# Ranking eight experts by token count and running three of them with both token parts in one stationary operand

## The chip, the core and the metric

The kernel runs on one core of one Trainium2 chip. The core has TensorE (PE in the rows; PEld is its weight load), VectorE (DVE), ScalarE (ACT), GpSimd (POOL) and SyncE (SP, which here issues the weight loads). The metric is the device time of one execution in microseconds (us). Before the change it is 1649.99 us, the median of three runs (1649.68 to 1650.12).

## The reference, cut to what matters

256 tokens of width 1024 go through two layers. Each layer has a mixer (attention, a gated delta rule and projections); the first is followed by a dense feed-forward part, the second by a mixture of eight experts. Only the experts are touched by the change:

```python
logits = xt @ router_w + router_b                    # 256 x 8
top_val, top_idx = lax.top_k(logits, 2)              # two experts for each token
gates = jax.nn.softmax(top_val, axis=-1)
# for each expert e, on the tokens that chose it:
gt, up = jnp.split(h @ w_gate_up[e], 2, axis=-1)     # 1024 -> 2 x 3584
y = (jax.nn.silu(gt) * up) @ w_down[e]               # 3584 -> 1024
x[token] += gate * y
```

Each expert holds 42 MiB of float32 weights, 336 MiB in all, and every expert's weights are used once. On the inputs of this case the reference's routing gives experts 0 to 7 these token counts: 42, 78, 96, 70, 54, 47, 76, 49.

## The kernel before

**Products in parts.** A float32 product is made of TensorE passes on a rounded type: a weight w is split into wh (rounded, written by ScalarE) and wl = w - wh (written by VectorE), and the activations likewise into a high and a low part. Three passes are added up in PSUM: high x wh, high x wl, low x wh. The activation is the stationary operand (128 columns: up to 128 tokens of one expert), the weights stream as 512 moving columns.

**Units and chunks.** A weight is loaded in units of 1 MiB (128 x 2048) by SyncE (`load`, L163 to L175). An expert has 7 chunks of 512 hidden columns; a chunk has 6 units: two of the gate half, two of the up half, two of the down projection. Each unit takes 12 matmuls, that is three for each of its four 128 x 512 blocks. `Weights` (L1023) keeps the order of units: `take(i)` asks for wh up to unit i+3 and wl up to unit i+2. Raw units have 12 buffers (NRAW = 5 and seven blocks), wh has 4 and wl has 3. A raw buffer comes free when its wl is written, so a load is issued then; a wl buffer comes free when TensorE has done the unit's matmuls.

**The loop over experts** (L1319 to L1344) runs expert after expert, chunk after chunk, in a fixed order on TensorE, ScalarE and VectorE (`pin`). For chunk c: the gate matmuls into pg (`gu`, L1239); ScalarE's silu of it to egt (L1325); the up matmuls into pu; VectorE's product egt (L1327); the down matmuls of the chunk before it into py (`finish`, `down`, L1250); four transposes of egt into pet (L1332); ScalarE's eah and VectorE's eal, the two parts of the turned activations (L1335, L1336).

**Tokens in and out.** `gather(e)` at chunk 1 builds a one-hot matrix GM from the tokens' slots (L1194), gets row numbers and gates by a small float32 matmul (pheld), and GpSimd fetches the expert's rows by an indirect transfer (xg, L1211). `turn` at chunk 4 transposes them to hTe in two parts. After an expert's last chunk `add_rows` scales py on ScalarE to ys and GpSimd adds the rows to acc in DRAM (L1270). Expert 0 gets its tokens by matmuls with GM, and experts 0 and 7 give their results back by matmuls (`scatter`). `gates` (L1158) makes the gates and the largest token count; if any expert has more than 128 tokens, the whole loop runs a second time for the rest (L1349).

Of the kernel before, what the change touches and what calls it, by code (L numbers as in the profile page):

```python
# [11 lines left out]
F32 = mybir.dt.float32  # L12
F32R = mybir.dt.float32r
# [5 lines left out]
P = 128  # L19
# [6 lines left out]
BESIDE = 16  # L26
# [17 lines left out]
K_COLS = K_KEPT + K_LEV + 128 * len(LEVELS)  # L44


def shape_constants():
# [10 lines left out]
    c[:, K_TOK:K_TOK + 4] = np.arange(P)[:, None] + np.array([0, P, S, 0])  # L58
    m = c[:, K_KEPT:]
# [8 lines left out]
class Even:  # L68
# [5 lines left out]
    def tile(self, shape, dtype, past=0, **kw):  # L74
        n = math.prod(shape[1:])
        if past:
            return self.pool.tile([shape[0], n + 64], dtype, **kw)[:, past:past + n].rearrange("p (a b) -> p a b", a=shape[1])
        return (self.small if n % 64 else self.pool).tile(shape, dtype, **kw)


def build(ctx, tc, nc, A, out, upto=99):
# [290 lines left out]
    def turned(pool, w, name, past=0):  # L372


        hh = pool.tile([P, KD, S], F32R, past=past, tag="hh", name=f"hh_{name}")
        hl = pool.tile([P, KD, S], F32R, past=past, tag="hl", name=f"hl_{name}")
# [73 lines left out]
    def mixer(l, mp):  # L450
# [500 lines left out]
        M = mp.tile([P, K_COLS - K_KEPT], F32, name="M")  # L951
        if l == 0:
            late_constants()
        nc.sync.dma_start(M, A["consts"][:, K_KEPT:])
# [6 lines left out]
    def ffn(l, fp):  # L961
        wg, wd = A["ffn_w_gate_up"], A["ffn_w_down"]
        with tc.high_priority():
            act = turned(fp, cols[:, V_FFN + 8 * l:V_FFN + 8 * l + 8], f"ffn{l}", 64 - BESIDE)
            _, rB = scales(fp)
# [49 lines left out]
    def moe(l, ep, wp, dram):  # L1015
# [7 lines left out]
        class Weights:  # L1023
# [36 lines left out]

        def sources(order):
            srcs, prev = [], None
            for e in order:
                wg, wd = A["moe_w_gate_up"][e], A["moe_w_down"][e]
                for c in range(nch):
                    srcs += [wg[2 * c + i] for i in range(2)] + [wg[14 + 2 * c + i] for i in range(2)] + (prev or [])
                    prev = [wd[2 * c + i] for i in range(2)]
            return srcs + prev

        W = Weights(sources(range(E)), "e")  # L1070
        W.hi(1, "c6")
        with tc.high_priority():
# [9 lines left out]
            xs = [ep.tile([P, D], F32, tag=f"xs{b}", name=f"xs{b}") for b in range(NB)]  # L1082
# [16 lines left out]
            def scores(b, n):  # L1099
# [6 lines left out]
                sq = ep.tile([P, 512], F32, tag="eah", bufs=2, name="nsq")  # L1106
# [40 lines left out]
        gate = ep.tile([P, NB, E], F32, name="gate")  # L1147

# [9 lines left out]
        def gates():  # L1158
            pcn = psb([P, E], "pcn")
            for b in range(NB):  # L1160
                mm(pcn, ones, sel[:, b, :], b == 0, b == NB - 1)
            cmax = ep.tile([P, 1], F32, name="cmax")
            V.tensor_reduce(cmax, pcn, axis=AX.X, op=ALU.max)
# [8 lines left out]
            V.tensor_tensor(gate, ex, mx[:, :, None].to_broadcast([P, NB, E]), op=ALU.mult)  # L1172
# [4 lines left out]
        def experts(off):  # L1177
            sl, xt = slot, xs
            if off:
                sl = ep.tile([P, NB, E], F32, name="slot2")  # L1180
                V.tensor_scalar(sl, slot, float(off), None, op0=ALU.subtract)
                xt = [ep.tile([P, D], F32, tag=f"xs{b}", name=f"xt{b}") for b in range(NB)]
                for b in range(NB):
                    nc.sync.dma_start(xt[b], xd[b * P:(b + 1) * P, :])
            ws = Weights(sources(range(E)), "o") if off else W
            used = [0]

            def gather(e):

                GM = ep.tile([P, NB, NS], F32, tag="GM", bufs=3, name="GM")  # L1190
                early = not off and e == 0
                for b in range(NB):
                    place = slot0[:, b, :] if early else sl[:, b, e:e + 1]
                    V.tensor_tensor(GM[:, b], iota0 if early else iota, place.to_broadcast([P, NS]), op=ALU.is_equal)  # L1194
                xg = rows = None
                if not off and e:

                    ph = psb([P, 3], "pheld")
                    for b in range(NB):
                        mm(ph, GM[:, b], held[:, b, e, :], b == 0, b == NB - 1)  # L1200
                    rows = ep.tile([P, 3], F32, tag="rows", bufs=3, name="rows")
                    V.tensor_copy(rows, ph)
                    ri = ep.tile([P, 2], I32, tag="ri", bufs=3, name="ri")
# [7 lines left out]
                    G.indirect_dma_start(out=xg, out_offset=None, in_=xd[:, :],  # L1211
                                         in_offset=bass.IndirectOffsetOnAxis(ap=ri[:, 0:1], axis=0))
# [227 lines left out]
```

## Time and profile before

| what | value |
|---|---|
| median of 3 runs | 1649.99 us |
| the profiled execution, its own time | 1650.56 us |
| its span, first to last instruction | 1648.8 us |
| TensorE busy in the span | 98% |
| VectorE busy | 82% |
| ScalarE busy | 65% |
| first gate matmul of expert 0 | 671.78 us after the span's start |
| mean rate of DMA, 800 to 1600 us | 380 GB/s |

The first 672 us are the two mixers, the dense part and the router; the last 977 us are the experts. In the rows each line is a group or a stretch of instructions: where a time stands first it counts from the span's start. TensorE's matmuls overlap, so the step from one start to the next, not the duration, tells how long one holds the engine.

### The profile page before, as it was taken

What the parts mean: (1) busy time and instruction counts of PE and PEld (TensorE: products, weight loads), DVE (VectorE), ACT (ScalarE), POOL (GpSimd) and SP (SyncE); (2) the same over time, 40 slices, a digit from 0 to 9 for tenths busy, and PEclk for the clock granted to TensorE, in tenths of its full rate; (3) what the DMA queues carried; (4) which work ended last, traced back from release to release, by engine and by line L of the source; (5) the groups of instructions that cost most, each with busy time, mean ns of one, the idle gap of its engine ahead of it and who ended that gap; (6) DMA issues with size and microseconds to landing.
All of it is one profiled execution on the core that took longest, in us unless ns stands there. A gap on an engine that the chain in (4) does not pass through costs nothing. (4 is left out here: it accounts for less than half of the span.)

```text
span 1648.8 us, 23472 instructions
## 1 busy us (share of the span) xinstructions
PE 1617.3 (98%) x9198; PEld 1402.8 (85%) x9198; DVE 1353.7 (82%) x1491; ACT 1069.4 (65%) x1124; POOL 96.3 (6%) x70
## 2 busy tenths in 40 slices
PE   8999999999999999899999999999999999999997
PEld 6899999999889997788788888888888888888885
DVE  6998776655799876789988888888888888888885
ACT  7555454444645554577777777777777777777773
POOL 0510000000051000000000000000100100000000
PEclk9999999999999999899999999999999999999998
DMA  7423455555442564699999999999999999999970
GB/s 291 156 100 143 155 185 197 180 189 195 142 140 103 183 252 155 258 375 370 365 391 358 383 397 364 382 391 370 381 390 364 393 382 356 408 365 376 400 308 28
DMA packets 67511, 466.61 MB, mean 283 GB/s; under 512 B 8000, under 2 KB 8512, under 8 KB 12608
## 3 DMA queue, kind: packets, MB, share of 16 engines
q1 hardware_dynamic: 64080, 453.95, 72.2%
q0 software_dynamic: 2160, 7.87, 1.7%
q10 hardware_dynamic: 1152, 3.21, 0.5%
q8 instruction: 74, 1.21, 0.3%
q14 instruction: 45, 0.37, 0.1%
HBM read 458.18 MB, written 6.82 MB: 282 GB/s over the span
## 5 line engine op out<-in xcount | busy, mean ns | idle before, releaser
L1052 DVE TENSOR_TENSOR wl_e<-raw,wh_e 128x2048 fp32r<-128x2048 f32 x336 | 753.4, 2284 | 7.5 <-PE pg L1237 1.8
L1039 ACT CAST wh_e<-raw 128x2048 fp32r<-128x2048 f32 x335 | 641.4, 1915 | 127.6 <-PE py L1237 37.8
L1237 PE MATMUL pg<-wh_e,hTe 128*128 128x512 f32 x896 | 293.0, 398 | 3.1 <-DVE hTe L1228 3.1
L1237 PE MATMUL pu<-wh_e,hTe 128*128 128x512 f32 x896 | 284.9, 389 | 0.0
L1237 PEld LDWEIGHTS pg<-wh_e,hTe 128*128 128x128 f32 x896 | 168.9, 189 | 38.6 <-DVE hTe L1228 3.7
L1237 PEld LDWEIGHTS pu<-wh_e,hTe 128*128 128x128 f32 x896 | 168.2, 188 | 34.9
L1237 PE MATMUL py<-wh_e,eal 128*128 128x512 f32 x448 | 175.3, 391 | 2.1 <-DVE eal L1336 2.1
L1237 PE MATMUL pg<-wl_e,hTe 128*128 128x512 f32 x448 | 175.8, 392 | 0.0
L1237 PE MATMUL py<-wh_e,eah 128*128 128x512 f32 x448 | 175.0, 391 | 0.5 <-ACT eah L1335 0.5
L1237 PE MATMUL py<-wl_e,eah 128*128 128x512 f32 x448 | 174.9, 390 | 0.0
L1237 PE MATMUL pu<-wl_e,hTe 128*128 128x512 f32 x448 | 174.3, 389 | 0.0
L1237 PEld LDWEIGHTS py<-wh_e,eal 128*128 128x128 f32 x448 | 84.5, 189 | 20.1 <-DVE eal L1336 2.6
L1237 PEld LDWEIGHTS py<-wh_e,eah 128*128 128x128 f32 x448 | 84.5, 189 | 18.2 <-ACT eah L1335 0.7
L1237 PEld LDWEIGHTS py<-wl_e,eah 128*128 128x128 f32 x448 | 84.5, 189 | 17.6
L1237 PEld LDWEIGHTS pu<-wl_e,hTe 128*128 128x128 f32 x448 | 84.1, 188 | 17.4
L318 PE MATMUL pf<-hh_ffn,wl_fg 128*128 128x256 f32 x352 | 98.8, 281 | 0.0
L1237 PEld LDWEIGHTS pg<-wl_e,hTe 128*128 128x128 f32 x448 | 84.7, 189 | 16.6 <-DVE wl_e L1052 0.3
L318 PE MATMUL pf<-hh_ffn,wh_fg 128*128 128x256 f32 x352 | 98.8, 281 | 0.0
L318 PE MATMUL pf<-hl_ffn,wh_fg 128*128 128x256 f32 x352 | 98.7, 281 | 0.0
L1336 DVE TENSOR_TENSOR eal<-pet,eah 128x512 fp32r<-128x512 f32 x56 | 38.7, 690 | 66.5 <-ACT eah L1335 66.5
L154 DVE TENSOR_TENSOR wl_fg<-raw,wh_fg 128x1024 fp32r<-128x1024 f32 x44 | 53.8, 1225 | 41.1 <-ACT wh_fg L153 41.0
L153 ACT CAST wh_fg<-raw 128x1024 fp32r<-128x1024 f32 x44 | 46.1, 1049 | 63.8 <-PE pf L318 37.5
(410 smaller groups left out, 2981.0 us busy)
## 6 DMA issues: line engine op xcount, KB each, us to landing
raw<-moe_w_gate_up SPq DMA_DIRECT2D x224, 1024.0 KB, 7.3
raw<-moe_w_down SPq DMA_DIRECT2D x112, 1024.0 KB, 7.7
raw<-w_in SPq DMA_DIRECT2D x43, 1024.0 KB, 4.8
raw<-ffn_w_gate_up SPq DMA_DIRECT2D x22, 1024.0 KB, 4.8
raw<-ffn_w_down SPq DMA_DIRECT2D x11, 1024.0 KB, 4.7
raw<-w_out SPq DMA_DIRECT2D x8, 1024.0 KB, 4.8
raw<-w_branch_b SPq DMA_DIRECT2D x4, 1024.0 KB, 4.8
raw<-w_branch_a SPq DMA_DIRECT2D x4, 1024.0 KB, 5.2
```

The source lines that it names most:

```text
L153: SC.copy(h[:, q], raw_ap[:, q])
L154: V.tensor_tensor(lo[:, q], raw_ap[:, q], h[:, q], op=ALU.subtract)
L318: T.matmul(o, lhsT, rhs, start=start, stop=stop)
L1039: pin(SC.copy(h, raw))
L1052: pin(V.tensor_tensor(w, raw, h, op=ALU.subtract))
L1237: pin(T.matmul(o, lhsT, rhs, start=start, stop=stop))
L1336: pin(V.tensor_tensor(al, pt_, ah, op=ALU.subtract))
```

## The change

**Ranking on chip.** `gates` counts tokens for each expert, ranks the experts by count and makes a permutation `at`: position q in the loop is no longer expert q. Expert 0 stays at position 0. The others are ranked by falling count, and `RANKS` puts the three with the fewest tokens at positions 2, 4 and 6. `gate` and `slot` are permuted to positions (`placed`). The number of the expert at each position, `who`, is read into registers of SyncE, and the loads of positions 1 to 7 take their address from such a register (`source`).

**Half experts.** At positions 2, 4 and 6 an expert may have at most 64 tokens. Its stationary operand holds the high parts of 64 tokens in columns 0 to 63 and their low parts in columns 64 to 127. Two passes, with wh and with wl, then give both parts' products in the two halves of the output rows. The halves of gate and up are copied out by ScalarE (egt, eup) and added and turned by eight float32 matmuls with `halves2`, two identity matrices on top of each other (pef); silu and product follow on 128 x 256 (esg), then the two parts (ea2). The two halves of py are added by two indirect transfers of 64 rows each. If a count is over its limit (64 or 128), the second run of the loop is taken, as before.

**Order.** Position 0 runs alone, then the chunks of positions 1 and 2 alternate (full, half, full, half), those of 3 and 4, of 5 and 6, and position 7 runs alone. Many buffers become single (egt, eah, eal), and xg and ys share one buffer.

```diff
+RANKS = (0, 1, 5, 2, 6, 3, 7, 4)
+HALF = P // 2
+def few(q):
+    return RANKS[q] >= 5
...
-                    raw = load(self.srcs[i])
+                    raw = load(source(*self.srcs[i]))
...
+        def source(name, q, u):
+            if number[q] is None:
+                number[q] = nc.values_load(who[0:1, q:q + 1], engines=[mybir.EngineType.SP], min_val=0, max_val=E - 1)
+            return A[name][number[q], u]
...
+        one = lambda q: [(q, c) for c in range(nch)]
+        pairs = one(0) + [(q + i, c) for q in range(1, E - 1, 2) for c in range(nch) for i in range(2)] + one(E - 1)
+        W = Weights(sources(pairs), "e")
...
+            V.tensor_tensor(at, cnt[:, 1, None, :].to_broadcast([P, E, E]), ranks[:, :, None].to_broadcast([P, E, E]), op=ALU.is_equal)
+            def placed(out, v):
+                V.tensor_tensor(gt[:, 0], at, v[:, None, :].to_broadcast([P, E, E]), op=ALU.mult)
+                V.tensor_reduce(out, gt[:, 0], axis=AX.X, op=ALU.add)
+            placed(cnt[:, 1], numbers)
+            V.tensor_copy(who, cnt[:, 1])
...
+            def products(o, parts, wh, wl, first, last):
+                if len(parts) == 1:
+                    mp(o, parts[0], wh, first, False)
+                    mp(o, parts[0], wl, False, last)
+                else:
+                    mp(o, parts[0], wh, first, False)
+                    mp(o, parts[0], wl, False, False)
+                    mp(o, parts[1], wh, False, last)
...
-                G.indirect_dma_start(out=acc[:, :], out_offset=bass.IndirectOffsetOnAxis(ap=ri[:, 1:2], axis=0),
-                                     in_=ys, in_offset=None, compute_op=ALU.add)
+                n = HALF if half else P
+                for r in range(0, P, n):
+                    G.indirect_dma_start(out=acc[:, :], out_offset=bass.IndirectOffsetOnAxis(ap=ri[0:n, 1:2], axis=0),
+                                         in_=ys[r:r + n, :], in_offset=None, compute_op=ALU.add)
...
+                if st["half"]:
+                    up = ep.tile([P, 512], F32, tag="eup", bufs=1, name="eup")
+                    pin(SC.copy(up, pu_))
+                else:
                     pin(V.tensor_tensor(g, pu_, g, op=ALU.mult))
...
+                    pt_ = psb([P, 2, 4, HALF], "pef")
+                    for i, r in enumerate((g, up)):
+                        for t in range(4):
+                            pin(T.matmul(pt_[:, i, t, :], r[:, t * P:(t + 1) * P], halves2, start=i + t == 0, stop=i + t == 4))
+                    sg = ep.tile([P, 4, HALF], F32, tag="GT", bufs=1, name="esg")
+                    pin(SC.activation(sg, pt_[:, 0], AF.Silu))
+                    pin(V.tensor_tensor(sg, pt_[:, 1], sg, op=ALU.mult))
```

How the instructions stand on VectorE in the middle of the expert loop, before: one chunk and a little more (wl_e is the low part of one unit).

```order
L1052 TENSOR_TENSOR wl_e_8726<-raw_8704,wh_e_8706 128x2048
L1052 TENSOR_TENSOR wl_e_8747<-raw_8722,wh_e_8724 128x2048
L1052 TENSOR_TENSOR wl_e_8765<-raw_8743,wh_e_8745 128x2048
L1327 TENSOR_TENSOR egt<-pu_8742,egt 128x512
L1052 TENSOR_TENSOR wl_e_8784<-raw_8761,wh_e_8763 128x2048
L1052 TENSOR_TENSOR wl_e_8802<-raw_8780,wh_e_8782 128x2048
L1336 TENSOR_TENSOR eal<-pet,eah 128x512
```

The product stands behind the fourth low part of the chunk's gate and up units, the activations' low part two units later. The same engine in the changed kernel, in one pair of a full and a half chunk (esg and ea2, here shown as ea, belong to the half chunk); six more wl_e follow the last row before the next esg.

```order
L1444 TENSOR_TENSOR esg<-pef,esg 128x256
L1071 TENSOR_TENSOR wl_e_8633<-raw_8597,wh_e_8599 128x2048
L1071 TENSOR_TENSOR wl_e_8651<-raw_8629,wh_e_8631 128x2048
L1449 TENSOR_TENSOR ea_8627<-esg,ea_8627 128x4x64
L1071 TENSOR_TENSOR wl_e_8674<-raw_8647,wh_e_8649 128x2048
L1071 TENSOR_TENSOR wl_e_8692<-raw_8670,wh_e_8672 128x2048
L1421 TENSOR_TENSOR egt<-pu_8669,egt 128x512
L1071 TENSOR_TENSOR wl_e_8711<-raw_8688,wh_e_8690 128x2048
L1071 TENSOR_TENSOR wl_e_8725<-raw_8707,wh_e_8709 128x2048
L1459 TENSOR_TENSOR eal<-pet,eah 128x512
```

VectorE still writes twelve wl_e for two chunks; the half chunk's product and low part have 256 columns instead of 512, and esg, which waits for pef, stands ahead of the third and fourth unit of the next full chunk.

TensorE before, where the down matmuls end and the next chunk's gate begins.

```order
L1237 MATMUL py_9074<-wl_e_9655,eah 128x512
L1237 MATMUL py_9074<-wh_e_9635,eal 128x512
L1332 MATMUL pet<-ident,egt 128x128 x4
L1237 MATMUL pg_9715<-wh_e_9653,hTe 128x512
L1237 MATMUL pg_9715<-wl_e_9674,hTe 128x512
L1237 MATMUL pg_9715<-wh_e_9653,hTe 128x512 x2
L1237 MATMUL pg_9715<-wl_e_9674,hTe 128x512
```

TensorE in the changed kernel at a like place: a half chunk's down matmuls (pya, pyb), the full chunk's transposes, the next half chunk's gate.

```order
L1307 MATMUL pyb<-wh_e_9866,ea_9821 128x512
L1307 MATMUL pyb<-wl_e_9896,ea_9821 128x512
L1456 MATMUL pet<-ident,egt 128x128 x4
L1307 MATMUL pg_9955<-wh_e_9894,hTe 128x512
L1307 MATMUL pg_9955<-wl_e_9915,hTe 128x512
L1307 MATMUL pg_9955<-wh_e_9894,hTe 128x512
L1307 MATMUL pg_9955<-wl_e_9915,hTe 128x512
```

The pass of the low part with wh is gone from the half chunk; each unit of a half expert holds 8 matmuls instead of 12.

## Rows read from the trace of the kernel before

**Rows 1.** The page, part 1: engine, busy us, share of span, instructions.

```profile
PE 1617.3 (98%) x9198; PEld 1402.8 (85%) x9198; DVE 1353.7 (82%) x1491; ACT 1069.4 (65%) x1124; POOL 96.3 (6%) x70
```

**Rows 2.** Stretch: PE, PEld, DVE, ACT, POOL busy; clock; DMA share; GB/s.

```profile
1000.00:1100.00 100.00, 100.00 (x454) 82.80 (x453) 89.18 (x57) 75.97 (x51) 2.57 (x2) 1.00 0.99 382
```

**Rows 3.** Groups by line, 800 to 1600 us: busy, mean ns, idle, releasers.

```profile
L1052 DVE TENSOR_TENSOR wl_e<-raw,wh_e 128x2048 fp32r<-128x2048 f32 x283 | 634.4, 2284 | 4.4 <-ACT wh_e L1039 0.5
L1039 ACT CAST wh_e<-raw 128x2048 fp32r<-128x2048 f32 x283 | 542.0, 1916 | 109.0 <-PE py L1237 32.9 <-PE pu L1237 30.4 <-PE pg L1237 18.5
...
L1336 DVE TENSOR_TENSOR eal<-pet,eah 128x512 fp32r<-128x512 f32 x47 | 32.5, 691 | 58.1 <-ACT eah L1335 58.1
...
L1228 DVE TENSOR_TENSOR hTe<-pgat,hTe 128x512 fp32r<-128x512 f32 x12 | 7.7, 680 | 0.0
```

**Rows 4.** Timeline of one chunk: start us, us, engine, line, operation.

```profile
999.55 0.48 PE L1237 MATMUL pg<-wh_e,hTe 128*128 128x512 f32 x1
...
1001.38 8.89 DVE L1052 TENSOR_TENSOR wl_e<-raw,wh_e 128x2048 fp32r<-128x2048 f32 x4
...
1010.56 0.39 PE L1237 MATMUL py<-wh_e,eah 128*128 128x512 f32 x1
...
1015.77 0.39 PE L1237 MATMUL py<-wh_e,eal 128*128 128x512 f32 x1
...
1016.36 0.48 PE L1237 MATMUL pg<-wh_e,hTe 128*128 128x512 f32 x1
```

**Rows 5.** The small float32 matmul pheld: count, ns min/median/max, first and last start.

```profile
L318 PE MATMUL pheld<-held,GM x28: 171/252/252, 706.5 to 1424.2; 128*128 128x3 f32 x28
```

**Rows 6.** Timeline at 706 us: four weight loads of two pheld calls.

```profile
706.44 0.53 PEld L318 LDWEIGHTS pheld<-held,GM 128*128 128x128 f32 x4
...
706.89 0.19 PEld L1237 LDWEIGHTS pg<-wh_e,hTe 128*128 128x128 f32 x1
```

**Rows 7.** SyncE's waits, 800 to 1600 us: total, times, longest.

```profile
SPq L173 <- DVE wl_e L1052: 681.4, 280, 8.1
```

**Rows 8.** Ten-us stretches after an expert's rows are added (columns as Rows 2).

```profile
1530.00:1540.00 10.00, 10.00 (x46) 8.26 (x45) 9.40 (x5) 7.28 (x6) 1.17 (x2) 1.00 1.01 350
1540.00:1550.00 10.00, 10.00 (x47) 8.27 (x46) 8.59 (x6) 7.58 (x6) 0.00 (x0) 1.00 1.02 426
...
1570.00:1580.00 10.00, 10.00 (x47) 8.28 (x46) 7.99 (x6) 6.83 (x6) 0.00 (x0) 1.00 1.02 428
```

**Rows 9.** Timeline of SyncE: one load's issue.

```profile
1058.35 0.33 SPq L173 DMA_DIRECT2D raw<-moe_w_down  x1
```

**Rows 10.** GpSimd's fetch of an expert's rows: ns min/median/max, first and last start.

```profile
L1211 POOL DMA_INDIRECT xg<-xd,ri x7: 956/992/3287, 708.7 to 1425.5; - x7
```

**Rows 11.** DMA issues, 800 to 1600 us: operation, count, median us to landing.

```profile
acc<-ys,ri POOLq DMA_INDIRECT x6, 10.3
```

**Rows 12.** Timeline from the router to expert 0's first chunk.

```profile
655.46 0.69 DVE L1075 TENSOR_SCALAR wn<-wn 128x1024 f32<-128x1024 f32 x1 [3.11 <-DMA wn<-norm_moe]
...
656.55 6.96 PE L318 MATMUL pl<-rw,hTr 128*128 128x8 f32 x32 [2.65 <-DVE rw L1080]
...
671.78 0.50 PE L1237 MATMUL pg<-wh_e,hTe 128*128 128x512 f32 x1
...
673.43 0.17 DVE L1172 TENSOR_TENSOR gate<-work,mx 128x16 f32<-128x16 f32 x1
...
678.87 1.03 PE L1237 MATMUL pg<-wh_e,hTe 128*128 128x512 f32 x2 [2.30 <-DVE hTe L1228]
...
682.26 0.52 PE L1237 MATMUL pg<-wl_e,hTe 128*128 128x512 f32 x1
```

**Rows 13.** A stretch of the second mixer (columns as Rows 2).

```profile
480.00:500.00 20.00, 17.82 (x144) 16.11 (x143) 19.97 (x36) 7.87 (x19) 8.90 (x6) 1.00 0.30 107
```

More of the change, by code (lines that the diff above doesn't have):

```diff
@@ L25 @@
 NRAW = 5
-BESIDE = 16
+BESIDE = 80
 IN_COLS = 5640
@@ L58, in shape_constants @@
     c[:, K_TOK:K_TOK + 4] = np.arange(P)[:, None] + np.array([0, P, S, 0])
+    c[:, K_POS:K_POS + 8] = RANKS
+    c[:, K_POS + 8:K_POS + 16] = [HALF if few(i) else P for i in range(N_EXP)]
+    c[:, K_POS + 16:K_POS + 24] = np.arange(N_EXP)
     m = c[:, K_KEPT:]
@@ L1298, in experts @@
             with tc.high_priority():
-                have = have()
+                have = {0: have()}
             if not off:
                 gates()
-            pend = None
+            pend, later = [], []
             def finish():
-                e, c, ah, al, py, GMe, rows = pend
-                down(e, c, ah, al, py)
+                st, e, c, act = pend.pop()
+                down(e, c, act, st["py"])
                 if c == nch - 1:
-                    if off or e == E - 1 or not rows:
-                        scatter(e, GMe, py)
+                    if st["rows"]:
+                        add_rows(st["rows"], st["half"], st["py"])
                     else:
-                        add_rows(rows, py)
+                        scatter(e, st["GT"], st["py"])
                     if not off and e == 0:
@@ L1317, in finish @@
                             nc.gpsimd.dma_start(x[:, b, :], acc[b * P:(b + 1) * P, :])
-            for e in range(E):
-                hTe, GMe, rows = have
-                py = None
-                for c in range(nch):
-                    pg_ = gu(hTe, f"g{e}")
-                    g = ep.tile([P, 512], F32, tag="egt", bufs=2, name="egt")
-                    pin(SC.activation(g, pg_, AF.Silu))
-                    pu_ = gu(hTe, f"u{e}")
-                    pin(V.tensor_tensor(g, pu_, g, op=ALU.mult))
-                    if pend:
-                        finish()
+            states, turns = {}, {}
@@ new lines, in experts, with parts @@
+            for v, (e, c) in enumerate(order):
+                if c == 0:
+                    hTe, GMe, rows = have.pop(e)
+                    half = not off and few(e)
+                    if off or e in (0, E - 1):
+                        rows = None
+                    states[e] = dict(hTe=hTe, GM=GMe, rows=rows, half=half)
+                st = states[e]
+                pg_ = gu(st["hTe"], st["half"], f"g{e}")
+                while later:
+                    later.pop()()
+                g = ep.tile([P, 512], F32, tag="egt", bufs=1, name="egt")
+                pin(SC.activation(g, pg_, AF.Copy if st["half"] else AF.Silu))
+                pu_ = gu(st["hTe"], st["half"], f"u{e}")
+                if st["half"]:
+                    up = ep.tile([P, 512], F32, tag="eup", bufs=1, name="eup")
+                    pin(SC.copy(up, pu_))
+                else:
+                    pin(V.tensor_tensor(g, pu_, g, op=ALU.mult))
+                todo = {} if not off else {1: ("get", e + 1), 4: ("turn", e + 1)}
+                if not off:
+                    if e == 0:
+                        todo = {1: ("get", 1), 3: ("turn", 1), 4: ("get", 2), 6: ("turn", 2)}
+                    elif st["half"]:
+                        todo = {1: ("get", e + 1), 3: ("turn", e + 1), 4: ("get", e + 2), 6: ("turn", e + 2)}
+                what, q = todo.get(c, (None, E))
+                if q < E and what == "get":
+                    turns[q] = gather(q)
+                elif q < E:
+                    have[q] = turns.pop(q)()
+                if pend:
+                    finish()
+                if st["half"]:
+                    pt_ = psb([P, 2, 4, HALF], "pef")
[5 more added lines that the diff above has]
+                    pin(V.tensor_tensor(sg, pt_[:, 1], sg, op=ALU.mult))
+                    a2 = ep.tile([P, 4, 2, HALF], F32R, tag="ea2", bufs=1, name="ea2")
+                    def parts(a2=a2, sg=sg):
+                        pin(SC.copy(a2[:, :, 0, :], sg))
+                        pin(V.tensor_tensor(a2[:, :, 1, :], sg, a2[:, :, 0, :], op=ALU.subtract))
+                    later.append(parts)
+                    act = [a2.rearrange("p t a s -> p t (a s)")]
+                else:
@@ L1379, in build @@
             nraw[0] = 0
+            over.tile([P, 384], F32, name="over")
             moe(1, Even(ep, es), wp, dram)
```

152 lines of the change are left out of this document (92 added, 60 removed).

## The prediction

> **What bounds the kernel now.** I read four views in this order. The page shows TensorE busy in 98% of the span [rows 1]; overlapping matmuls fill such a share easily, so the stretches decide. In a stretch inside the experts TensorE is busy all the time at clock 1.00, the upper of its two levels (2.4 GHz; the lower is 1.2), VectorE for 89% and ScalarE for 76% [rows 2]. The groups show who waits: ScalarE's casts wait for TensorE (32.9, 30.4 and 18.5 us after py, pu and pg), while VectorE's low parts wait for almost nothing (4.4 us in 800) and follow on the casts [rows 3]. So TensorE sets the pace of the experts and VectorE is close behind. The timeline gives the pace: a chunk runs from 999.55 to 1016.36, 16.81 us; 24 down matmuls start in 1010.56 to 1015.77, so one step is 5.21 / 23 = 0.2265 us and 72 steps are 16.31, which leaves 0.50 for the four transposes. VectorE writes four low parts in 8.89 us, 2.22 each, 13.3 for the six of a chunk, plus two of 0.69 [rows 4, 3]. With the work at an expert's change, expert follows expert every (1424.2 - 706.5) / 6 = 119.6 us [rows 5], 1.9 more than seven chunks. Two chunks of different experts therefore take 2 x 119.6 / 7 = 34.17 us now; that is the unit of my sum.
>
> **TensorE's part of a pair.** A half chunk has 48 steps instead of 72: 10.87 us. Its four transposes are replaced by eight float32 matmuls of 64 columns. No row has these; the nearest is pheld, whose two float32 calls stand in the trace as four weight loads and hold TensorE from 706.44 to 706.89, 0.1125 us each [rows 6]. Eight calls are then 16 x 0.1125 = 1.8 us. That price is bounded below by the transposes (0.5) and above by 16 matmuls at the full step (3.6); I take 1.8, since pheld has the same kind of stationary operand and even fewer columns. So a half chunk is 12.67, and a full and a half one together 29.48 us. The work at an expert's change stays (1.9 x 2 / 7 = 0.55 a pair): 30.0 us against 34.17. If all of it arrives, 21 pairs bring 21 x 4.1 = 87 us.
>
> **What becomes late.** VectorE's low parts stay twelve a pair: 26.7 us, plus 0.69 x 2 for the full chunk and, estimated at half of that for half the columns, 0.7 for the half one, plus some 0.7 for row numbers and hTe, 29.4 in all. That fits in 30.0 on the average, not in detail. Only three low parts can be ahead, and a half expert's unit lasts 8 x 0.2265 = 1.81 us on TensorE, less than the 2.22 that VectorE needs for the next. I walked through one pair from the rows (time 0 is the full chunk's first gate matmul, units 0 to 11 in order of use). Full gate and up, units 0 to 3: 0 to 10.87, no wait. VectorE's product egt, queued behind unit 5, is done at 11.7. The half down units 4 and 5 last to 14.50, the transposes to 15.0. VectorE writes units 6 and 7 until 16.2, eal until 16.8 (it waits for ScalarE's eah), then units 8, 9 and 10, done at 19.05, 21.3 and 23.5. TensorE would want unit 8 at 18.6: it waits 0.45, then 0.4 for unit 9 and 0.4 for unit 10. Full down units 10 and 11 last to 28.9, the float32 matmuls to 30.7. esg waits for them, and behind it on VectorE stand the next full chunk's units 2 and 3, wanted 5.4 and 8.2 us later, so nothing more is lost there and the full chunk refills the lead. The waits are 1.25 us a pair. Of VectorE's 0.7 for hTe and row numbers I count half as lying in the same short stretch. A pair is 30.0 + 1.25 + 0.35 = 31.6 us, 2.57 less than now: 21 x 2.57 = 54 us. Positions 0 and 7, fourteen full chunks, keep their 16.81.
>
> **ScalarE** gets two copies of 512 columns, a silu and a cast of 256 for a half chunk; twelve casts of 1.9 and these are some 27 of 31.6 us. It stays behind VectorE, at no price of its own.
>
> **Transfers.** A pair needs 12 units, 12.58 MB. At the present 382 GB/s [rows 2] that is 32.9 us, more than 31.6. But that rate is what the loads are asked for, not what they can do: every load waits for VectorE to free its buffer (280 times, 681 us) [rows 7]. After an expert's rows are added, the loads catch up at 426 to 428 GB/s for 40 us [rows 8]; at 426 a pair takes 29.5. Need is 374 now, so those 40 us made up 2.1 MB, about 5 us for each expert's fetch and add; 10 us for two experts, 1.4 a pair, makes 30.9. That is under 31.6. Should it be over, twelve raw buffers, filled in expert 0, cover it: ten units of 2.46 us are 25 us of lead, 1.2 us for each of 21 pairs. So transfers bind only above 32.8 a pair. The Trainium skill ("DMA: Bandwidth & Descriptors", Bandwidth) says that between HBM and SBUF a limit of about 358 GB/s for each core binds; by it a pair would take 35.1 us, more than now, and this change would lose 21 x 1.0 = 21 us. The trace differs: 382 and 426 were measured. Its page "HBM Reference", Specifications, gives about 425 for a core that streams alone, and with that the trace agrees.
>
> **Loads by register.** SyncE issues a load in 0.33 us [rows 9] and needs one every 2.6; the changed order has one more instruction ahead of each load. Even GpSimd's median issue with row numbers, 0.99, fits [rows 10]; its longest, 3.29, would not. The eight register reads stand behind the thirteenth load and wait for `who`, some 5 us after the first gate matmul; behind them wait only loads that are wanted 30 us later. I take nothing.
>
> **One buffer for xg and ys.** A half expert's ys must wait until the full one's rows have landed, 10.3 us after their issue [rows 11]; between the two evictions lie pef (1.8), the next full chunk's 48 gate and up steps (10.9) and the half one's 16 down steps (3.6), 16 us less the copy to ys. Covered; if the landing took 20 us, three stalls of up to 6 would cost 18.
>
> **Start.** Some 24 small VectorE operations come into `gates`; at 0.17 us, which one of its present ones takes [rows 12], or a little less where they follow each other closely, they put 3 to 4 us in front of the second low part; but hTe's second low part, for which TensorE waited until 678.87, now stands ahead of them, and the router's constants wn and rw (waits of 3.11 and 2.65) are loaded earlier. Between 6 gained and 5 lost I take 2 gained.
>
> **Sum.** 54 + 2 = 56 us off the profiled execution's 1650.56; against the median 1649.99 the same difference gives 1594.
>
> **Rivals.** *The hand-over costs nothing* (lead always full, pair at 30.0): 1650 - 87 - 2 = 1561. Against it: VectorE is left with 0.6 us in 30. *Transfers bind*: a mean of 400 GB/s instead of 426, from more small indirect packets, makes 31.5 + 1.4 = 32.9, about the forecast with the lead gone; 380 makes 34.5, and with the lead's 25 us 1650 + 7 - 25 - 2 = 1630. At 358, 21 x (35.1 + 1.4 - 34.17) = 49 us come on and the lead's 25 off: 1672; I leave that 0.01, since 382 is measured over a stretch of 100 us. (It is the rate of the Trainium skill's rule above.) For a binding transfer: DMA's busy share is 0.99 already [rows 2]. *TensorE's clock*: waits could come in lumps. After the wait of 2.30 us the next eight matmuls took 3.39 us to 682.26, steps of 0.42, which is the lower level, 1.6 us lost [rows 12]. One such fall in each pair costs 34: 1628. Against it: a mixer stretch with TensorE busy 17.82 of 20 us kept 1.00 [rows 13], and my waits are 0.45 at most. *Slower: register loads issue slowly.* Position 1 to 7 have 294 loads; each may take 119.6 / 42 = 2.85 us before the present pace is lost. At GpSimd's 3.29 they take 967 us instead of 837: 1780. Against it: there is one more instruction, not a list of rows. *It doesn't do what it says*: a third-smallest count above 64 takes the second run, 8 x 119.6 = 957 us more, 2607; the reference's counts at those positions are 54, 49 and 47, so ten tokens are missing.
>
> **Chances.** Forecast 0.55 (1580 to 1610 for itself), hand-over free 0.12, transfers 0.15 (0.01 of it at 358), clock 0.07, slow register loads 0.04, second run 0.01, other losses that eat the gain 0.06. A change under 0.2%, 3.3 us, is about what a measurement of this kernel can't tell from none. Faster: all of the first four but 0.03, and a little of the others: 0.88; same 0.05; slower 0.07. The range goes from near the free hand-over, 1565, to the clock and transfer cases, 1632.
>
> **What would show it.** Right: half units' steps of 0.2265, pef near 1.8 us, pairs of some 31.6 us, TensorE's waits for wl_e in the half chunks, clock 1.00, loads above 400 GB/s in 800 to 1500 us, SyncE still waiting for wl_e. Wrong: ScalarE's casts waiting for raw loads (transfers), granted clock below 1 among the pairs, SyncE's issues of over 2.6 us, or a second run after position 7.

## The result, and the profile after

The changed kernel takes 1584.81 us (median of 4 runs, 1583.25 to 1585.29) against 1650.05 for the kernel before beside it (4 runs, 1649.68 to 1650.62): a ratio of 0.9603, with a 95% interval of 0.9588 to 0.9619. That is 65.2 us less, where 56 were forecast; the time lies within the range, 9 us under the forecast. The profiled execution took 1585.29 us with a span of 1583.5.

First the page, part 1, and the long stretches inside the pairs (columns as in [rows 2]):

```profile
PE 1545.5 (98%) x8946; PEld 1329.4 (84%) x8946; DVE 1339.2 (85%) x1515; ACT 1069.5 (68%) x1166; POOL 115.3 (7%) x76
```

```profile
880.00:980.00 100.00, 97.52 (x454) 78.46 (x453) 93.19 (x60) 81.59 (x61) 2.31 (x1) 1.00 0.99 402
980.00:1080.00 100.00, 99.04 (x472) 80.75 (x471) 93.03 (x62) 82.01 (x64) 10.58 (x4) 1.00 1.01 413
1080.00:1180.00 100.00, 97.95 (x458) 79.42 (x457) 93.11 (x59) 80.59 (x61) 2.51 (x1) 1.00 1.01 418
1280.00:1380.00 100.00, 99.41 (x467) 80.74 (x465) 95.11 (x60) 83.36 (x63) 4.58 (x1) 1.00 1.01 426
```

The share of TensorE's busy time over the span, 98%, is the one of [rows 1]: it says nothing of the 65 us. The stretches do. Before, TensorE was busy for all of 100 us and VectorE for 89 [rows 2]; now TensorE has gaps of 0.6 to 2.5 us in 100 and VectorE is at 93 to 95. The granted clock is 1.00 in all of them, the upper level.

How long a pair of chunks takes is read from the new float32 matmuls, of which each pair has one set, and from ScalarE's silu behind them (esg), one for each pair. These are two rows of the view of one tile, pef (count, ns min/median/max, first and last start):

```profile
L1441 PE MATMUL pef<-halves,egt x168: 217/275/276, 827.2 to 1448.0; 128*128 128x64 f32 x168
L1443 ACT ACTIVATE esg<-pef x21: 385/385/387, 829.2 to 1449.2; 128x256 f32<-128x256 f32 x21
```

168 matmuls are eight for each of 21 pairs, and from the first esg to the last are 20 pairs: (1449.2 - 829.2) / 20 = 31.00 us a pair, the work at the experts' changes included. (The expectations below say 31.04: that counts from the first matmul of the first set to the last one of the last set, which is 0.04 too long.) Before it was 34.17, from [rows 5]. 21 x (34.17 - 31.00) = 66.6 us: the whole gain is here.

The waits between 800 and 1440 us (total, times, longest) show what TensorE still waits for, and who does not wait:

```profile
PEld pu L1307 <- DVE wl_e L1071: 17.5, 29, 1.9
PEld py L1307 <- DVE wl_e L1071: 9.3, 18, 0.7
...
ACT wh_e L1058 <- DMA raw<-moe_w_gate_up: 0.8, 1, 0.8
```

PEld is the weight load. Where these waits lie can be seen in the timeline of weight loads of one pair (the end of a row is the idle time before it, and its releaser):

```profile
973.90 0.19 PEld L1307 LDWEIGHTS pu<-wl_e,hTe 128*128 128x128 f32 x1 [0.43 <-DVE wl_e L1071]
...
976.10 0.19 PEld L1307 LDWEIGHTS pu<-wl_e,hTe 128*128 128x128 f32 x1 [0.51 <-DVE wl_e L1071]
...
978.31 0.19 PEld L1307 LDWEIGHTS py<-wl_e,eah 128*128 128x128 f32 x1 [0.52 <-DVE wl_e L1071]
```

The full chunk's transposes in this pair stand at 969.39 and its half chunk's float32 matmuls at 983.66; so these are the half chunk's two up units and the first of the two down units of the full chunk that follow: units 8, 9 and 10 of the walk in the prediction. What TensorE loses by the second of them is seen in its own timeline:

```profile
975.62 0.39 PE L1307 MATMUL pu<-wh_e,hTe 128*128 128x512 f32 x1
976.11 0.50 PE L1307 MATMUL pu<-wl_e,hTe 128*128 128x512 f32 x1
976.44 0.39 PE L1307 MATMUL pu<-wh_e,hTe 128*128 128x512 f32 x1
```

From start to start it is 0.49 and 0.33 where two steps of 0.2265 would be 0.45: 0.37 lost, less than the 0.51 of the weight load's wait: where nothing waits, a weight load starts one step ahead of its matmul (979.12 and 979.34). The other two cost 0.29 and 0.37; the three 1.03 us.

The pairs are not all alike. TensorE's timeline has pef in four pairs that follow each other, and the work at an expert's change between them (pgat turns the fetched rows, pheld makes the row numbers for the next fetch):

```profile
889.13 1.00 PE L1441 MATMUL pef<-halves,egt 128*128 128x64 f32 x8
...
906.14 0.60 PE L1291 MATMUL pgat<-ident,xg 128*128 128x128 f32 x4
910.24 0.60 PE L1291 MATMUL pgat<-ident,xg 128*128 128x128 f32 x4
919.74 1.00 PE L1441 MATMUL pef<-halves,egt 128*128 128x64 f32 x8
...
936.76 0.50 PE L333 MATMUL pheld<-held,GM 128*128 128x3 f32 x4
953.05 1.00 PE L1441 MATMUL pef<-halves,egt 128*128 128x64 f32 x8
...
983.66 1.00 PE L1441 MATMUL pef<-halves,egt 128*128 128x64 f32 x8
```

The last pair is a plain one, 30.61 us. The first, with the turn, takes no longer: 30.61. The second, with the row numbers, takes 33.31. VectorE's timeline shows what happens there: the copy of the row numbers stands ahead of the next low part, and VectorE idles 1.76 us until TensorE has done pheld; TensorE then waits twice, 1.02 and 0.96 us, for low parts.

```profile
933.26 2.28 DVE L1071 TENSOR_TENSOR wl_e<-raw,wh_e 128x2048 fp32r<-128x2048 f32 x1
937.30 0.16 DVE L1270 COPY rows<-pheld 128x3 f32<-128x3 f32 x1 [1.76 <-PE pheld L333]
```

The same wait of 1.76 us stands once more, in the pair between the esg at 1139.80 and at 1172.90, 33.10 us. The other 18 of the 20 pairs take 30.61 to 31.25.

The DMA view of the same stretch gives 411 GB/s (382 before [rows 2]):

```profile
DMA packets 36817, 262.76 MB, mean 411 GB/s; under 512 B 4127, under 2 KB 4127, under 8 KB 5407
```

### The profile page after: what moved, and what is told of

It is laid out like the page before. It is cut to its first block, busy times and chain, and to the rows that moved or that the text cites. A ratio compares the mean times of both kernels' runs of the same rounds, so it can differ in the third digit from the quotient of the medians.

```text
span 1583.5 us, 23686 instructions
## 1 busy us (share of the span) xinstructions
PE 1545.5 (98%) x8946; PEld 1329.4 (84%) x8946; DVE 1339.2 (85%) x1515; ACT 1069.5 (68%) x1166; POOL 115.3 (7%) x76
## 4 chain that ended last, share of the span: by engine, by line
PE 88%; DVE 7%; DMA 2%; ACT 2%; issue 1%; POOL 0%; ACTq 0%; DVEq 0%; SPq 0%
PE pg L1307 16%; PE pu L1307 15%; PE py L1307 12%; PE pf L333 8%; PE pd L333 4%; DVE wl_e L1071 3%; PE p_ga L333 3%; PE p_gb L333 3%; PE pef L1441 2%; PE pyb L1307 2%; PE pya L1307 2%; PE p_wo L333 2%; PE p_z L333 1%; PE p_cq L333 1%; PE p_ya L333 1%; PE p_yb L333 1%
## 5 line engine op out<-in xcount | busy, mean ns | idle before, releaser
L1307 PE MATMUL pg<-wh_e,hTe 128*128 128x512 f32 x728 | 251.0, 399 | 0.0
L1307 PE MATMUL pu<-wh_e,hTe 128*128 128x512 f32 x728 | 244.2, 390 | 0.0
L1307 PE MATMUL py<-wl_e,eah 128*128 128x512 f32 x280 | 111.3, 397 | 2.1 <-DVE wl_e L1071 1.0
L1307 PE MATMUL py<-wh_e,eah 128*128 128x512 f32 x280 | 109.4, 391 | 0.7 <-ACT eah L1458 0.7
L1307 PE MATMUL py<-wh_e,eal 128*128 128x512 f32 x280 | 109.4, 391 | 0.0
L333 PEld LDWEIGHTS pf<-hh_ffn,wh_fg 128*128 128x128 f32 x704 | 108.2, 188 | 0.8
L1307 PEld LDWEIGHTS py<-wl_e,eah 128*128 128x128 f32 x280 | 52.5, 188 | 20.3 <-DVE wl_e L1071 9.8
L333 PEld LDWEIGHTS pf<-hh_ffn,wl_fg 128*128 128x128 f32 x352 | 67.4, 192 | 0.0
L1307 PEld LDWEIGHTS py<-wh_e,eah 128*128 128x128 f32 x280 | 52.6, 188 | 12.9 <-ACT eah L1458 0.9
L1307 PEld LDWEIGHTS py<-wh_e,eal 128*128 128x128 f32 x280 | 52.6, 188 | 10.7 <-DVE eal L1459 0.4
```

What stands on the lines that cost most here:

```text
L333: T.matmul(o, lhsT, rhs, start=start, stop=stop)
L1307: pin(T.matmul(o, lhsT, rhs, start=start, stop=stop))
```

## The experiments

Each is compared with the kernel before in the same session; the changed kernel's own ratio, 0.9603 [0.9588, 0.9619], is the mark. 0.001 in the ratio is 1.65 us.

**What the two passes are worth without the rest, and the rest without them.** Two things came together in the change. The first experiment makes every expert a full one, in the order of before (one position after the other), and leaves all that goes with the ranking:

```
-    return RANKS[q] >= 5
+    return False
...
-    pairs = one(0) + [(q + i, c) for q in range(1, E - 1, 2) for c in range(nch) for i in range(2)] + one(E - 1)
+    pairs = [v for q in range(E) for v in one(q)]
...
-    if e == 0:
-        todo = {1: ("get", 1), 3: ("turn", 1), 4: ("get", 2), 6: ("turn", 2)}
+    if True:
+        todo = {1: ("get", e + 1), 4: ("turn", e + 1)}
```

> No expert is half: all eight run with three passes, one after the other as in the kernel before, but ranked on chip, with loads addressed by the register, one buffer each for eah, eal, egt and one for xg and ys. It is the price of everything but the two passes. Theory (these cost nothing on the path, and the start is 3.2 us shorter): 1650 - 3 = 1647, between 1644 and 1651. Rival (the registers, the single buffers or the shared xg buffer cost some us per expert which the gain of the passes covers): 1655 to 1670.

Measured: 1645.93 us, ratio 0.9974 [0.9963, 0.9985], so 4.3 us less than before (2.5 to 6.1). In its trace the scatter of expert 0 stands at 803.6 us, 5.1 earlier than before (808.7): what the start gains comes through, and no cost of ranking, registers, single buffers and the buffer that xg and ys share is seen beside it. The other 61 us are the two passes' and their order's.

**Addresses without a register.** `number` is written as `[0, 2, 4, 1, 7, 6, 5, 3]`, the experts at the eight positions:

```
-        number = [0] + [None] * (E - 1)
+        number = [0, 2, 4, 1, 7, 6, 5, 3]
```

> The order of the experts is written into the kernel (the one that the ranking finds for these inputs), so loads have constant addresses; the ranking is still worked out, nothing waits for its result. Theory (a register load on SyncE is hidden by the lead of the raw buffers): 1585, between 1582 and 1587. Rival (the wait for the ranking and the register reads delay loads): 1570 to 1580.

Measured: 1584.22 us, ratio 0.9598 [0.9582, 0.9614]: no difference that can be told. The changed kernel's timeline of SyncE shows why: a load is issued in 0.33 us as before [rows 9], with a move of 0.03 ahead of it:

```profile
L188 SPq DMA_DIRECT2D raw<-moe_w_gate_up x151: 332/333/337, 859.8 to 1439.7; - x151
L188 SPq MOVE raw<-moe_w_gate_up x150: 29/29/37, 863.5 to 1438.1; - x150
```

**VectorE's low parts, cut.** If TensorE waits for low parts, a kernel with shorter ones shows TensorE's own pace:

```
+    m = UNIT // 2 if name == "moe_w_gate_up" and few(q) else UNIT
-    pin(V.tensor_tensor(w, raw, h, op=ALU.subtract))
+    pin(V.tensor_tensor(w[:, 0:m], raw[:, 0:m], h[:, 0:m], op=ALU.subtract))
...
-    products(ps, parts, wh[:, kk, :], wl[:, kk, :], k == 0, k == KD - 1)
+    products(ps, parts, wh[:, kk, :], wl[:, kk % 2 if half else kk, :], k == 0, k == KD - 1)
```

> In half chunks the low parts of the four gate/up units are taken over half of their columns only, and the matmuls read these columns twice (the low part of the other half of these weights is left out). VectorE's work falls by about 4 x 1.15 = 4.6 us in a pair of 31.04, TensorE's, ScalarE's and the transfers' work is as it was. Theory (TensorE waits for low parts, some 1.3 us in a pair by the trace of after: 17.5 + 9.3 us from 800 to 1440): 1585 - 21 x 1.3 = 1558, between 1552 and 1566. Rival 1 (transfers bind: VectorE waits only where data are late): 1580 to 1586. Rival 2 (the path is TensorE's work alone, the waits are covered by something else that comes next, such as esg through ScalarE): 1575 to 1585.

Measured: 1562.49 us, ratio 0.9468 [0.9452, 0.9484], 22.3 us less than the changed kernel. Its esg and two of its stretches:

```profile
L1445 ACT ACTIVATE esg<-pef x21: 385/385/385, 827.9 to 1426.6; 128x256 f32<-128x256 f32 x21
```

```profile
880.00:980.00 100.00, 100.00 (x484) 83.48 (x483) 83.91 (x62) 83.25 (x62) 1.24 (x1) 1.00 1.01 419
1280.00:1380.00 100.00, 100.00 (x476) 83.63 (x475) 85.05 (x57) 83.83 (x63) 0.00 (x0) 1.00 1.01 426
```

TensorE is full again, with a pair of (1426.6 - 827.9) / 20 = 29.94 us. That is the price of TensorE's part alone; the changed kernel's 31.00 has 1.06 us of VectorE's hand-over in it, 21 x 1.06 = 22.3. Both rivals fall. It was less than the 1.3 that I had read from PEld's waits, since TensorE does not lose all of such a wait. A plain pair takes 29.53 us here (ScalarE's esg starts at 1397.06 and 1426.58), so the waits cost one 30.61 - 29.53 = 1.08. The transfers followed at 419 to 426 GB/s.

**Half the bytes.** The same cut on the loads' side: the half experts' gate/up units are loaded to half, and both casts read these columns twice.

```
+    brief = self.srcs[i][0] == "moe_w_gate_up" and few(self.srcs[i][1])
-    raw = load(source(*self.srcs[i]))
+    raw = load(source(*self.srcs[i]), UNIT // 2 if brief else UNIT)
+    if brief:
+        raw = raw[:, None, 0:UNIT // 2].to_broadcast([P, 2, UNIT // 2])
...
```

> The gate/up units of the three half experts are loaded to half (columns 0 to 1023 of 2048), and the casts read these columns twice; the other half of these weights is left out. All engines do the same number of instructions of the same size, and 4 x 0.5 = 2 MiB of the 12.6 MB of a pair are not moved. Theory (transfers wait for buffers, not the reverse: 539 us of the queue's waits for low parts from 800 to 1440, 0.8 us of waits for raw units): 1585, between 1581 and 1587. Rival (the transfers are late, as VectorE's waits could hide): 1563 to 1575, what the shorter low parts gave back.

Measured: 1581.63 us, ratio 0.9587 [0.9572, 0.9601]. At 339 to 355 GB/s instead of 402 to 426 in the four stretches the time is the same or some 3 us less; the intervals overlap the changed kernel's. So the transfers, at DMA shares of 0.99 to 1.01, did not set the pace. (The 539 us of the queue's waits in the expectation were counted from 660 us; from 800 to 1440 they are 447.)

The trace shows where the 3 us lie. The two pairs with the row numbers take 31.21 and 30.80 us here instead of 33.31 and 33.10, 4.4 us less together; every other pair is within 0.05 of the changed kernel's. In these two the copy of the row numbers stands behind one more low part and no longer waits:

```profile
932.65 4.49 DVE L1075 TENSOR_TENSOR wl_e<-raw,wh_e 128x2048 fp32r<-128x2048 f32 x2
937.05 0.15 DVE L1274 COPY rows<-pheld 128x3 f32<-128x3 f32 x1
```

The kernel does not fix this copy's place (it has no `pin`), and it differs from kernel to kernel. No run moved the copy alone, so that its place is worth these 4 us is read from two traces, not shown by an edit.

**No alternation.** The half experts stay half, but the positions run one after the other:

```
-    pairs = one(0) + [(q + i, c) for q in range(1, E - 1, 2) for c in range(nch) for i in range(2)] + one(E - 1)
+    pairs = [v for q in range(E) for v in one(q)]
```

> The eight positions run one after the other, all seven chunks of one, then all seven of the next; the three half experts stay half (2 passes), ranking and loads by register stay. Theory (TensorE and VectorE both matter, and the alternation lets VectorE's even load of six low parts per chunk run beside an uneven load of TensorE): a half chunk alone is then bound by VectorE, 6 x 2.28 + 0.42 + 0.42 = 14.5 us and some 0.2 of the expert's own low parts, against some 12.6 of TensorE (48 x 0.2265 + 1.7); with a full chunk's 17.1 that makes 31.7 to 32.0 for two chunks against 31.04 now, so 1585 + 21 x 0.65 to 0.95: 1599 to 1605 us. Rival 1 (the alternation gives nothing, the sum of TensorE's work decides): 1585 +- 3. Rival 2 (transfers bind the half chunks, 15.4 us each at the mean of 411 GB/s): 21 x 1.5 more, about 1616.

Measured: 1583.05 us, ratio 0.9594 [0.9578, 0.9610]. My theory fell, the first rival stood: with this number of buffers the alternation gives nothing that can be told. VectorE's timeline of one half chunk (start, us) shows where the theory's number was wrong:

```profile
955.12 2.28 DVE L1071 TENSOR_TENSOR wl_e<-raw,wh_e 128x2048 fp32r<-128x2048 f32 x1
957.32 0.41 DVE L1444 TENSOR_TENSOR esg<-pef,esg 128x256 f32<-128x256 f32 x1
957.65 4.48 DVE L1071 TENSOR_TENSOR wl_e<-raw,wh_e 128x2048 fp32r<-128x2048 f32 x2
962.05 0.42 DVE L1449 TENSOR_TENSOR ea<-esg,ea 128x256 fp32r<-128x256 f32 x1
962.39 4.49 DVE L1071 TENSOR_TENSOR wl_e<-raw,wh_e 128x2048 fp32r<-128x2048 f32 x2
966.79 1.28 DVE L1298 TENSOR_TENSOR hTe<-pgat,hTe 128x512 fp32r<-128x512 f32 x2
```

A low part is recorded with 2.28 us, but the next instruction starts 2.20 after it; esg and ea take 0.33 and 0.34 from start to start. A half chunk alone needs 6 x 2.20 + 0.67 = 13.87 us of VectorE. The next two rows show the period, by ScalarE's timeline:

```profile
946.48 0.41 ACT L1448 CAST ea<-esg 128x256 fp32r<-128x256 f32 x1
956.78 0.39 ACT L1443 ACTIVATE esg<-pef 128x256 f32<-128x256 f32 x1 [1.70 <-PE pef L1441]
960.67 0.41 ACT L1448 CAST ea<-esg 128x256 fp32r<-128x256 f32 x1
970.65 0.39 ACT L1443 ACTIVATE esg<-pef 128x256 f32<-128x256 f32 x1 [0.41 <-PE pef L1441]
```

From esg to esg it is 13.87. VectorE does bind a half chunk in turn, as the theory said, but at 13.87 us where it stands alone and 14.37 in the mean of six with the work at the change (86.24 us), not at 14.7. From the first esg of position 2 (928.24) to that of position 6 (1362.58) lie 14 full and 14 half chunks: 31.02 us a pair, what the alternated order reaches too (31.00). The changed kernel's two waits of 1.76 us are not in this order (its copies of row numbers wait 0.5 us in all), so up to some 4 us of a gain by the alternation may be hidden in the comparison.

**A fourth buffer of low parts.** If the alternated pair's 1.06 us are a lack of lead and not of VectorE's rate (12 x 2.20 + some 1.9 = 28.3 of 29.94), one buffer more must bring some of it, and in turn it must bring nothing. The block c5 goes from the raw ring to the low parts; the second kernel has the sequential `pairs` of the experiment above besides.

```
-    ring[:] = ["c3", "c1", "c2", "c0", "c4", "c5", "c6"] + [None] * NRAW
+    ring[:] = ["c3", "c1", "c2", "c0", "c4", "c6"] + [None] * NRAW
...
-    if i % 3 == 0:
-        w = block("c7", f"wl_{self.name}{i}", dtype=F32R)
+    if i % 4 in (0, 2):
+        w = block(("c7", "c5")[i % 4 // 2], f"wl_{self.name}{i}", dtype=F32R)
...
-    self.lo(i + 3)
+    self.lo(i + 4)
```

> One buffer of 128x2048 goes from the raw ring (12 to 11) to the low parts (3 to 4), and low parts are made one unit further ahead; all work is the same. Theory (in the alternated order VectorE has 12 x 2.20 + some 1.9 = 28.3 us of work in a pair against TensorE's 30.0, so TensorE's waits of 1.06 us in a pair are lack of lead, which one more buffer gives): 1567 to 1577, of the 22 us that shorter low parts gave back at least 8. Rival 1 (VectorE's rate decides, lead does not help): 1583 to 1587. Rival 2 (a raw buffer less costs more than the low buffer brings): above 1587.

> The positions run one after the other, with four buffers of low parts and eleven raw ones. Theory (in turn, a half chunk stands alone and VectorE needs 6 x 2.20 + 0.33 + 0.34 = 13.9 us for it against TensorE's 12.6, so its rate decides there and lead cannot help; only in the alternated order does a buffer more pay): 1578 to 1584, within 5 us of 1583 with three buffers, and some 10 above the alternated order with four (1571). Rival (the alternation is worth nothing, the buffer alone brings the 14 us): 1569 to 1574.

Measured: 1570.84 us, ratio 0.9518 [0.9504, 0.9533], in the alternated order; 1584.54 us, ratio 0.9602 [0.9587, 0.9616], in turn. Both go as the theory says (the second 0.5 us above its range): the buffer alone brings nothing, the alternation alone nothing that can be told, the two together 14 us. Two stretches of the alternated kernel, and a half and a full expert of the one in turn:

```profile
1080.00:1180.00 100.00, 99.93 (x477) 82.86 (x476) 96.14 (x61) 83.70 (x61) 2.31 (x1) 1.00 1.01 423
1280.00:1380.00 100.00, 99.88 (x481) 83.06 (x480) 96.53 (x57) 82.16 (x61) 0.00 (x0) 1.00 1.01 427
```

```profile
930.00:1015.00 85.00, 81.99 (x408) 65.82 (x407) 84.32 (x65) 76.02 (x66) 10.42 (x3) 1.00 1.01 413
1040.00:1150.00 110.00, 110.00 (x508) 91.35 (x506) 98.09 (x58) 83.99 (x56) 3.42 (x2) 1.00 1.01 417
```

In turn, 930 to 1015 lies in a half expert: VectorE is busy 84.32 of 85 us and TensorE 81.99; 1040 to 1150 in a full one: TensorE 110 of 110, VectorE 98. One engine binds, then the other. Alternated with enough lead, both run at 96 to 100%. The alternated kernel's pair is (1436.0 - 831.8) / 20 = 30.21 us:

```profile
L1443 ACT ACTIVATE esg<-pef x21: 385/385/387, 831.8 to 1436.0; 128x256 f32<-128x256 f32 x21
```

21 x (31.00 - 30.21) = 16.6 us; its first esg stands 2.6 later than the changed kernel's, which leaves 14. A plain pair takes 29.88 (30.61 in the changed kernel): that is the lead. Some 4 of the 16.6 us lie beyond that in the two pairs with the row numbers, whose copy does not wait here either.

**The start.** In the changed kernel the first low parts stand behind the ranking on VectorE. TensorE's timeline, the stretch of 20 us around it, and two shorter ones within:

```profile
675.64 0.79 PE L1307 MATMUL pg<-wl_e,hTe 128*128 128x512 f32 x1 [4.21 <-DVE wl_e L1071]
```

```profile
660.00:680.00 20.00, 15.55 (x70) 13.75 (x70) 16.56 (x51) 9.11 (x10) 0.00 (x0) 0.74 0.49 169
662.00:668.00 6.00, 5.76 (x29) 5.70 (x28) 3.69 (x13) 5.79 (x4) 0.00 (x0) 0.50 0.29 89
676.00:678.00 2.00, 2.00 (x6) 1.52 (x6) 2.00 (x2) 0.00 (x0) 0.00 (x0) 0.50 0.42 53
```

The clock of 0.74 holds two falls to the lower level: one ahead of the wait, one right after it.

One kernel works the ranking out after the first chunk's gate matmuls (and keeps its scratch in the buffer of eup); a second has four buffers of low parts besides:

```
+    if not off and v == 0:
+        gates()
     while later:
```

> The ranking of the experts and the gates are worked out after the first chunk's gate matmuls in place of ahead of the first units' low parts; the rest is the same. Theory (at the start of the experts TensorE waited 4.2 us for the first low parts behind the ranking on VectorE, and its clock fell for 3 us after that): 1585 - 4 to 6, so 1579 to 1581. Rival (the ranking's small operations come between later low parts and TensorE waits there, with no lead yet): 1583 to 1586.

> The two edits together: four buffers of low parts with eleven raw ones, and the late ranking. Theory: the sum of the two gains, 1585 - 8 to 18 - 4 to 6: 1561 to 1573. Rival (either gains nothing): 1579 or more.

Measured: 1582.45 us, ratio 0.9590 [0.9575, 0.9605] with three buffers of low parts, between the theory and the rival and not told apart from the changed kernel; 1573.04 us, ratio 0.9531 [0.9518, 0.9544] with four, at the upper end of what was expected and not below four buffers alone. The two gains do not add up. The wait has moved (with four buffers the longest is 6.6 us, for egt); this is the late ranking with three buffers:

```profile
671.83 0.50 PE L1307 MATMUL pg<-wl_e,hTe 128*128 128x512 f32 x1 [0.21 <-DVE wl_e L1071]
...
684.26 1.11 PE L1456 MATMUL pet<-ident,egt 128*128 128x128 f32 x4 [4.43 <-DVE egt L1421]
```

4.21 us at the first low part became 4.43 at the transposes, which wait for VectorE's product egt; it stands on VectorE behind the ranking and the low parts made ahead. A last kernel makes fewer low parts ahead in the first two chunks, with the ranking after the whole first chunk:

```
-    self.lo(i + 3)
+    self.lo(i + (2 if i < 4 else 3 if i < 10 else 4))
```

> Four buffers of low parts and eleven raw ones; the ranking comes after the whole first chunk, and the low parts run only two units ahead in the first chunk, three in the second and four from there. Theory (with the late ranking alone the wait moved from the first low part to the first gate-up product, which stands on VectorE behind low parts made ahead; with less lead at the start it is ready earlier): 1571 - 3 to 6, so 1565 to 1568. Rival (VectorE has at the start the same work to do before TensorE can run on, wherever the waits lie): 1569 to 1574.

Measured: 1570.32 us, ratio 0.9516 [0.9503, 0.9529]: the rival. The wait for egt is 0.85 us now, and others have come, in the second chunk:

```profile
678.11 0.66 PE L1454 MATMUL pet<-ident,egt 128*128 128x128 f32 x4 [0.85 <-DVE egt L1419]
...
684.89 0.36 PE L333 MATMUL pheld<-held,GM 128*128 128x3 f32 x2 [2.69 <-DVE held L1241]
686.99 0.80 PE L1307 MATMUL pg<-wl_e,hTe 128*128 128x512 f32 x1 [1.74 <-DVE wl_e L1071]
```

Moving the ranking or the lead about moves the wait. The runs fit with VectorE's work at the start being what is short: in the wait of 4.21 us VectorE is busy 3.93 of the 4 us from 671.5 to 675.5, in the wait of 4.43 all 4 us from 680 to 684. But no run took that work away, so this is argued, not shown.

The kernels with four buffers of low parts, at 1570.84 and 1570.32 us, are the fastest with the whole result: 14 us under the changed kernel and 80 under the one before.

## Why the prediction was right, step by step

The forecast's mechanism held: TensorE's part shrinks, VectorE's hand-over takes some of it back, the transfers do not become late. One term of the sum was too large by more than half.

- **TensorE's part of a pair.** Put at 30.0 us, measured 29.94 in the kernel with short low parts. The float32 matmuls, priced at 1.8 us from pheld [rows 6], take 1.70: in one pair they start at 1014.39 and the next gate matmul at 1016.09, 0.106 for each of 16. The neighbour row was a good price, and its bounds of 0.5 and 3.6 were not needed.
- **VectorE's hand-over in a plain pair.** Forecast 29.48 + 1.25 = 30.73 us, measured 29.53 + 1.08 = 30.61. The walk through a pair was right in place and near in size: it had waits of 0.45, 0.4 and 0.4 for units 8, 9 and 10, and TensorE lost 0.29, 0.37 and 0.37 there. Its price of 2.22 for a low part, four in a row divided by four, was near the 2.20 from start to start, which is what counts.
- **The work at an expert's change.** This is the term that was mis-sized: 0.55 for TensorE and 0.35 for VectorE, 0.90 a pair; measured 31.00 - 30.61 = 0.39 in the changed kernel, and 29.94 - 29.53 = 0.41 with short low parts, where almost nothing waits for VectorE. The forecast added TensorE's extra work to the waits, as if it came beside them. In a pair with the turn it falls into them: with short low parts that pair is 0.90 longer than a plain one (esg at 887.32 and 917.75, 30.43 us), in the changed kernel it is 30.61 like the plain one; that TensorE's turn gives VectorE the time to come up is the likely reason, not one that a run shows. Two pairs with the row numbers go the other way, 33.31 and 33.10. The forecast had VectorE's operations there, but not that VectorE would stand idle for TensorE's pheld: of the 2.70 us of the first pair 1.76 are this wait and 0.87 the small operations.
- **The pair.** Forecast 31.63, measured 31.00; 21 x 0.63 = 13 us, of which 11 by the change's term. One us of it was lost again at the start and some 3 around the first and the last pair, which no view here explains; that leaves the 9 us between forecast and time. That the forecast missed by 9 and not by 13 is luck.
- **The start.** Forecast 2 us gained, between 6 gained and 5 lost. The first up matmul starts 3.2 us earlier (679.63 after, 682.85 before), though the wait that the forecast feared is there, 4.21 us for a low part behind the ranking. Only 1.1 us of it is left at expert 0's scatter (807.6 after, 808.7 before; why the rest goes stays open). Between the two scatters, of expert 0 and of the last position, lie 766.9 us, 831.0 before: 64.1, which with the 1.1 makes the 65.2.
- **Transfers.** The forecast let them bind above 32.8 us a pair. They did not at 31.00 (one wait of ScalarE's casts for a raw unit, 0.8 us), nor at 29.94. The rate was 411 GB/s in the mean over 640 us, and 426 to 427 in stretches, what the loads had reached when they caught up [rows 8]; taking away half of the half experts' gate/up bytes left every pair but the two with the row numbers as it was. The Trainium skill ("DMA: Bandwidth & Descriptors", Bandwidth) puts the binding limit between HBM and SBUF at about 358 GB/s a core; the 411 of this kernel, which runs on one core, go against it. "HBM Reference", Specifications, of the same skill gives about 425 for one core that streams alone, which the stretches at 426 to 427 agree with.
- **Registers, and the shared buffer.** Put at nothing. Fixed addresses change nothing that can be measured, and all experts full, with registers and shared buffers, is 4 us faster than before, the earlier start included.
- **The clock.** The rival of falls in each pair is refuted: 1.00 in all four stretches. Around the start of the experts it fell to the lower level twice, from 662 to 668 us and after the wait of 4.21 us.
- **What the prediction did not ask.** It took the alternated order as given and never priced the pair in turn. That order was worth nothing that can be told with three buffers of low parts and 14 us with four.

## What to carry to other kernels

When one engine's work in a stage shrinks, walk through one unit of the pattern with the buffers' number in hand: the average of the next engine (28.3 of 30.0 us here) says that the gain fits, the walk says how much of it the lead lets through. Interleaving a stage that one engine binds with a stage that another binds paid here only when the buffers between them held the surplus; try order and depth together, since each alone showed nothing. And look where a small operation that waits for another engine stands in its queue: here such a copy, one low part too early, held VectorE for 1.76 us twice.

## What the runs showed of the hardware

- Neighbouring VectorE instructions overlap in the records by about 0.08 us: 2.28 recorded for a 128x2048 low part, 2.20 from start to start; 0.42 and 0.34 for a cast's low part of 256 columns.
- A float32 matmul with 64 columns is two weight loads and two matmuls in the trace; the eight calls of a half chunk are 16 of each, 0.106 us each.
- DMA's busy share stood at 0.99 to 1.01 at 402 GB/s and at 426, and at 0.91 to 0.94 at 339 to 355: a share near 1 did not mean that the engines waited for data.
- The granted clock fell to its lower level twice around the start of the experts in the changed kernel: 0.50 from 662 to 668 us, after TensorE was busy for 2.53 of the 4 us from 656 to 660, and 0.50 from 676 to 678, after the wait of 4.21 us. With the late ranking the second fall goes with the wait: 1.00 in every 2 us from 670 to 682, about 0.5 from 682 to 688 (the wait of 4.43 us ends at 684.26), 0.83 in this stretch:

```profile
680.00:700.00 20.00, 15.74 (x64) 13.02 (x65) 16.83 (x18) 10.05 (x7) 2.85 (x1) 0.83 0.92 327
```
